# Beginning the accumulating transfers a seven sooner, and a first feed-forward block whose last pair is a seven

## The chip, the cores and the metric

The kernel runs on one core of one Trainium2 chip. The metric is the device time of one execution in microseconds (us), taken as the median of several runs. Five engines work side by side, each through its own instructions in the order in which they were written: TensorE (PE, matrix multiplications), VectorE (DVE), ScalarE (ACT), GpSimd (POOL), and SyncE (SP), which here does little else than issue loads. A transfer that is issued by SP or POOL is carried out by 16 DMA engines, which the queues share.

## The reference

One decoder layer for 256 tokens of width 2048, in float32: a SwiGLU feed-forward (half weight) with layer norm, two token mixers side by side (chunked retention, and sliding-window attention with sinks) with layer norm, a second such feed-forward with layer norm, and a gated per-layer embedding with layer norm. The change touches the two feed-forwards only, the first one most.

```python
def swiglu(x, w_gu, w_down):              # w_gu 2048 x 11264, w_down 5632 x 2048
    g, u = jnp.split(x @ w_gu, 2, axis=-1)
    return (jax.nn.silu(g) * u) @ w_down

h = x                                     # 256 x 2048
h = layer_norm(alpha * h + 0.5 * swiglu(h, w_ffn1_gu, w_ffn1_down), ln_g[0], ln_b[0])
...
h = layer_norm(alpha * h + 0.5 * swiglu(h, w_ffn2_gu, w_ffn2_down), ln_g[2], ln_b[2])
```

## The kernel before, in words

**Three products for one.** A float32 matrix is held as a rounded high part and the low rest, and a product is summed as low·high + high·high + high·low (L431 to L433, three matmuls of 128x128 by 128x512). Every weight chunk (512 KB, 128 x 1024 numbers) is loaded by SP into a slot (L119, tile `r...`), ACT casts the high part (L105, tile `h...`), and DVE subtracts it from the raw chunk for the low part (L106, tile `l...`). Slots come from one pool of 46.

**Units of a block.** The first matrix of a feed-forward (`gu`) is done in 11 blocks `j` of 512 columns of g and of u; each block sums over 8 pairs of K-chunks, and each pair is a unit. The second matrix (`down`) is done in two blocks of 22 pairs (`f1d`, then `f1e`; `f2d` and `f2e` in the second feed-forward). A string of letters gives the kinds of a block's units:

- `P`, plain: 24 matmuls; two chunks, each with a cast on ACT and a subtraction on DVE.
- `S`, a seven: seven products instead of eight (a Strassen form), so 21 matmuls. DVE forms four sums of the two chunks (L226 to L229, tiles `u` and `v`), ACT casts what comes out, and DVE makes the four low parts (`l`, `b`, `lu`, `lv`). At the end of a block that has sevens, a fold (L549 to L553) combines four extra accumulators `s0` to `s3`: ACT copies `s0`, and DVE does four sums over `evw` and `eve`. The left operands of the sevens are sums of x ("forms", L504 to L507 and a split, tiles `sums`, `f1fh`, `f1fl`), made once for a group of two pairs.
- `F`, folded: as `P`, but the low part of the second chunk isn't made by DVE. ACT writes the negated raw chunk, rounded, into the low tile (L169), POOL issues a transfer that adds the raw chunk onto it in memory (L170, an accumulating transfer), and ACT then casts the high part (L171).

**Order.** The program is written out by a planner, `fill`: it takes units from a list `plan`, loads them while their work in the queue is under a bound and slots are left, and "makes" them (casts, sums, subtractions) some time before PE needs them. `slots_for_weights` sets how many slots it may use. All engines then run strictly in the order that results. Eight PSUM banks go round: with sevens in two neighbouring blocks, the accumulators of a block use the banks that `s0` to `s3` of the block ahead of it held, so the first matmuls of a block wait for the fold of the block before.

**Start.** The first block of the first feed-forward begins while x and the weights are still arriving. x comes in four chunks, in order 0, 1, 2, 3, each ahead of the weights that meet it; block 0 takes pairs 0 to 7 as `P`, with 9 slots for weights, and 24 from unit 6 on. Both groups of forms are made at unit 7. A block without sevens is evicted with two activations and two multiplications (L1062 to L1064); one with sevens takes the fold, four additions (L1056), an activation (L1057) and a multiplication (L1058), after which the result is turned (L185 to L196).

Of the kernel before, what the change touches and what calls it, by code (L numbers as in the profile page):

```python
# [16 lines left out]
P = 128  # L17
# [34 lines left out]
SECOND_DOWN = "PPPSPSPSFSPSFSSPSPPPPP"  # L52
# [10 lines left out]
def layer(ctx: ExitStack, tc: tile.TileContext, io):  # L63
# [89 lines left out]

    class Folded:

        loads, makes, keeps, time = 1, 2, 2, 12

        def __init__(self, key):  # L160
            self.key = key

        def load(self, **how):
            self.chunk = Chunk(self.key, **how)

        def make(self):
            c = self.chunk
            c.make_hi()
            act.mul(c.lo, c.raw, -1.0)  # L169
            pool.dma_start(c.lo, c.raw, accum_op=ALU.add)  # L170
            act.copy(c.hi, c.raw)  # L171

    class Turn:
# [142 lines left out]
    def fill(must=False):  # L316

        while True:
            queued = sum(u.time for u in ready)
            left = room["slots"] - room["used"]  # L320
            wanted = must and not ready or not room["quiet"] and queued < room["ahead"]
            if loaded and wanted and loaded[0].makes <= left:
                u = loaded.pop(0)
                u.make()
                room["used"] += u.keeps - u.loads
                ready.append(u)
                continue
            first = loaded[0] if loaded else plan[0] if plan else None
            queued += sum(u.time for u in loaded)
            if plan and queued < room["far"] and plan[0].loads + first.makes <= left:  # L330
                u = plan.pop(0)
                u.load()
                room["used"] += u.loads
                loaded.append(u)
                continue
            return

    def make_next():
# [4 lines left out]
        ready.append(u)  # L343

    def take(key):
        if not ready:
            fill(True)
# [626 lines left out]
    def ffn(name, i, ht, norm, keep, residual, keepers, away):  # L974
# [33 lines left out]
        for j in range(KF // 4):  # L1008
# [22 lines left out]
            def before(u, j=j, offset=KD // 2 - len(units)):  # L1031
                u += offset
                if j == 0 and norm is None and u % 2 == 0:
                    first_chunk(u // 2)
                    if u == 6:
                        slots_for_weights(24)
                    if u == 2:
                        load_constants()
                if j == 0 and u == 7:
                    for g in sorted({p // 2 for p in SEVEN}):  # L1040
                        hi, lo = (slot([P, 8, P], F32R, f"{name}f{w}{g}") for w in "hl")
                        made[g] = seven_forms(keep[g], hi, lo)
                    if name == "f2":
                        g = AHEAD[1][0] // 2
                        made[g] = forms_of([ht[:, 4 * g : 4 * g + 4, :]], f"{name}f{g}")
# [733 lines left out]
    def first_chunk(c):  # L1779
# [4 lines left out]
        if c < 3:  # L1784
            load_x_chunk(c + 1)

# [157 lines left out]
```

## Time and profile before

| | us |
|---|---|
| median of three runs | 2230.45 |
| runs | 2227.97, 2230.45, 2230.84 |
| the profiled execution's own time | 2230.62 |
| its span, first to last instruction | 2228.6 |
| PE busy | 2218.5 |
| DVE busy | 2004.0 |
| ACT busy | 1439.0 |

The span is what the trace covers; the execution's own time is 2.0 us longer for what lies around it. Matmuls overlap (a row lists some 0.39 us, and the next starts earlier), so the pace of PE is read from the starts of neighbouring rows and not from the durations. The granted clock of PE is 0.999 over the span. In the rows of a timeline stand: start, duration, engine, line, operation, output <- inputs, shape and count, and in square brackets the idle time just ahead with what ended it. Tile names there leave out numbers: `lf_gu` is any low chunk of the first matrix of either feed-forward.

### The profile page before, as it was taken

Reading aid. Unit: us, or ns where it says so; the run is one execution under the profiler, and the core shown is the slowest. Engines: PE = TensorE matmul, PEld = TensorE weight load, DVE = VectorE, ACT = ScalarE, POOL = GpSimd, SP = SyncE. Lnnn points to the kernel's source line nnn. Section 1 sums busy time; section 2 is a strip of 40 time slices with the busy share of each in tenths; the row PEclk is TensorE's granted clock in tenths of the full one; section 3 lists DMA queues with packets and bytes.
Section 4 is the critical chain, followed back from the end, with each engine's and each line's share of the span. In section 5 each row is a group of like instructions: output and inputs, shape, how many; then the busy total and the mean of one; then the engine's idle time right before and its main releaser. Section 6 shows DMA issues by size and latency. Waiting matters only on the chain.

```text
span 2228.6 us, 29103 instructions
## 1 busy us (share of the span) xinstructions
PE 2218.5 (100%) x10140; PEld 1838.9 (83%) x10140; DVE 2004.0 (90%) x2624; ACT 1439.0 (65%) x1677; POOL 50.9 (2%) x65
## 2 busy tenths in 40 slices
PE   9999999999999999999999999999999999999998
PEld 8888888888888888888788888888888888888887
DVE  6999999989998789789999888779999999999977
ACT  6777777777565545557865567466766677765653
POOL 0000000000000000000000000000000000000000
PEclk9999999999999999999999999999999999999999
DMA  9988998976686889757976568888999999666871
GB/s 321 250 264 252 249 263 241 269 227 217 228 305 234 298 283 338 203 179 232 291 233 226 184 203 321 316 302 266 301 301 295 300 248 276 209 233 221 309 283 68
DMA packets 302075, 570.51 MB, mean 256 GB/s; under 512 B 98652, under 2 KB 103388, under 8 KB 301928
## 3 DMA queue, kind: packets, MB, share of 16 engines
q1 hardware_dynamic: 291880, 536.71, 72.3%
q0 software_dynamic: 8064, 29.36, 7.0%
q10 hardware_dynamic: 1984, 2.58, 0.4%
q8 instruction: 79, 1.29, 0.2%
q14 instruction: 68, 0.56, 0.1%
HBM read 487.32 MB, written 31.46 MB: 233 GB/s over the span
## 4 chain that ended last, share of the span: by engine, by line
PE 93%; DMA 3%; DVE 2%; issue 1%; ACT 0%; SPq 0%; ACTq 0%; POOL 0%; DVEq 0%; POOLq 0%
PE rqk L382 3%; PE f2g L431 3%; PE f2g L433 3%; PE f2g L432 3%; PE f1g L431 2%; PE f1g L433 2%; PE f1g L432 2%; PE f2u L431 2%; PE f2u L433 2%; PE f2u L432 2%; PE f1u L433 2%; PE f1u L431 2%; PE f1u L432 2%; PE aqk L382 2%; PE f2e L431 1%; PE f1e L431 1%
## 5 line engine op out<-in xcount | busy, mean ns | idle before, releaser
L106 DVE TENSOR_TENSOR lf_gu<-rf_gu,hf_gu 128x1024 fp32r<-128x1024 f32 (+1 forms) x225 | 267.7, 1210 | 22.1 <-ACT hf_gu L105 21.1
L105 ACT CAST hf_gu<-rf_gu 128x1024 fp32r<-128x1024 f32 (+1 forms) x225 | 228.7, 1039 | 22.1 <-DMA rf_gu<-in_f_gu 21.5
L106 DVE TENSOR_TENSOR lw_in_f<-rw_in_f,hw_in_f 128x1024 fp32r<-128x1024 f32 x140 | 167.8, 1219 | 15.0 <-ACT hw_in_f L105 15.0
L106 DVE TENSOR_TENSOR lf_down<-rf_down,hf_down 128x1024 fp32r<-128x1024 f32 x130 | 155.7, 1220 | 12.9 <-ACT hf_down L105 11.1
L105 ACT CAST huf_gu<-uf_gu 128x1024 fp32r<-128x1024 f32 x76 | 80.1, 1053 | 125.4 <-DVE uf_gu L227 109.4
L105 ACT CAST hf_down<-rf_down 128x1024 fp32r<-128x1024 f32 x130 | 132.7, 1049 | 30.5 <-DMA rf_down<-in_f_down 21.3
L105 ACT CAST hw_in_f<-rw_in_f 128x1024 fp32r<-128x1024 f32 x140 | 140.4, 1049 | 2.3 <-PE gt L433 1.6
L105 ACT CAST hvf_gu<-vf_gu 128x1024 fp32r<-128x1024 f32 x76 | 80.1, 1054 | 32.4 <-DVE vf_gu L229 30.5
L106 DVE TENSOR_TENSOR luf_gu<-uf_gu,huf_gu 128x1024 fp32r<-128x1024 f32 x76 | 92.6, 1218 | 0.0
L106 DVE TENSOR_TENSOR lvf_gu<-vf_gu,hvf_gu 128x1024 fp32r<-128x1024 f32 x76 | 92.6, 1218 | 0.0
L431 PE MATMUL f1g<-hf_gu,xt 128*128 128x512 f32 x232 | 90.8, 391 | 0.0
L433 PE MATMUL f1g<-lf_gu,xt 128*128 128x512 f32 x232 | 90.5, 390 | 0.0
L432 PE MATMUL f1g<-hf_gu,xt 128*128 128x512 f32 x232 | 90.5, 390 | 0.0
L431 PE MATMUL f2g<-hf_gu,ht 128*128 128x512 f32 x211 | 82.2, 390 | 0.0
L433 PE MATMUL f2g<-lf_gu,ht 128*128 128x512 f32 x211 | 82.1, 389 | 0.0
L432 PE MATMUL f2g<-hf_gu,ht 128*128 128x512 f32 x211 | 82.1, 389 | 0.0
L433 PE MATMUL f1u<-lf_gu,xt 128*128 128x512 f32 x192 | 75.0, 391 | 1.2 <-DMA lf_gu<-rf_gu 1.2
L431 PE MATMUL f1u<-hf_gu,xt 128*128 128x512 f32 x192 | 74.7, 389 | 0.0
L432 PE MATMUL f1u<-hf_gu,xt 128*128 128x512 f32 x192 | 74.7, 389 | 0.0
L170 POOL DMA_DIRECT2D lf_gu<-rf_gu x42 | 36.4, 867 | 1641.2 <-DMA rf_gu<-in_f_gu 1017.6
L105 ACT CAST huf_down<-uf_down 128x1024 fp32r<-128x1024 f32 x32 | 33.7, 1054 | 60.7 <-DVE uf_down L227 58.7
L1057 ACT ACTIVATE eve<-eve 128x1024 f32<-128x1024 f32 x20 | 21.2, 1061 | 67.3 <-DVE eve L1056 67.3
(1512 smaller groups left out, 6978.3 us busy)
## 6 DMA issues: line engine op xcount, KB each, us to landing
rf_gu<-in_f_gu SPq DMA_DIRECT2D x361, 512.0 KB
rf_down<-in_f_down SPq DMA_DIRECT2D x176, 512.0 KB
rw_in_f<-in_w_in_f SPq DMA_DIRECT2D x148, 512.0 KB
lf_gu<-rf_gu POOLq DMA_DIRECT2D x42, 512.0 KB, 8.2
rw_rv<-in_w_rv SPq DMA_DIRECT2D x32, 512.0 KB
rw_ret<-in_w_ret SPq DMA_DIRECT2D x32, 512.0 KB
rw_mix<-in_w_mix SPq DMA_DIRECT2D x32, 512.0 KB
rw_pg<-in_w_pg SPq DMA_DIRECT2D x32, 512.0 KB
```

The lines of the kernel that those rows point to most:

```text
L105: act.copy(dst_hi, src)
L106: (lo_engine or dve).tensor_tensor(dst_lo, src, dst_hi, ALU.subtract)
L170: pool.dma_start(c.lo, c.raw, accum_op=ALU.add)
L382: pe.matmul(ps[f], hi[:, kk, f * P : (f + 1) * P], rhs(k), start=k == 0, stop=k == n_k - 1,)
L431: pe.matmul(o, al, bh, start=first, stop=False)
L432: pe.matmul(o, ah, bh, start=False, stop=False)
L433: pe.matmul(o, ah, bl, start=False, stop=self.left == 0)
L1057: act.activation(g, g, AF.Silu)
```

## The change

1. The accumulating transfer of an `F` is split off. A unit `Folding` (load, negation, transfer) is put into the plan ahead of the work it follows, by at least 12 of the planner's matmul units and back to the start of a seven where one is near; a unit `Folded` at the old place only casts the high part.
2. Block 0 of the first feed-forward takes pairs 0, 1, 4, 5, 6, 7, 2 as `P` and then pair 3 as a seven. x is loaded in order 0, 2, 3, 1. The forms of group 1 are made at unit 6, those of group 0 at unit 7. The slots go from 9 to 16 at unit 4 and to 28 at unit 6.
3. Block 1 of the first feed-forward is `FFSSFSSF` and not `FFSSFSSP`.
4. The first `down` block of both feed-forwards has another order, with six `F` instead of five and eight `S` as before.

```diff
+FOLD_AHEAD = 12, 12
+FORMS_AT = {"f1": {6: (1,), 7: (0,)}, "f2": {7: (0, 1, 2)}}
+FIRST_SLOTS = {4: 16, 6: 28}
+X_ORDER = (0, 2, 3, 1)
+FIRST_UNITS = {
+    "f1": [('P', 0), ('P', 1), ('P', 4), ('P', 5), ('P', 6), ('P', 7), ('P', 2), ('S', 3)],
+    "f2": [('P', 0), ('P', 1), ('P', 2), ('P', 3), ('P', 4), ('P', 5), ('P', 6), ('P', 7)],
+}
-FIRST_DOWN = "PPPPPPFFSFSPSFSPSFSSPS"
+FIRST_DOWN = "PPPPPFFSFSFSPSFSPSFSPS"
...
-    class Folded:
-        loads, makes, keeps, time = 1, 2, 2, 12
+    class Folding:
+        loads, makes, keeps, time = 1, 1, 2, 0
...
         def make(self):
             c = self.chunk
-            c.make_hi()
+            c.lo = slot(list(c.raw.shape), F32R, "l" + c.name)
             act.mul(c.lo, c.raw, -1.0)
             pool.dma_start(c.lo, c.raw, accum_op=ALU.add)
+
+    class Folded:
+        loads, makes, keeps, time = 0, 1, 2, 12
...
+        def make(self):
+            c = self.chunk = self.begun.chunk
+            c.hi = slot(list(c.raw.shape), F32R, "h" + c.name)
             act.copy(c.hi, c.raw)
+            room["used"] -= self.begun.keeps
+
+    def fold_at(ahead, key):
+        begun = Folding(key)
+        at, time = len(plan), 0
+        while at > 0 and time < ahead:
+            at -= 1
+            time += plan[at].time
+        if ahead and any(isinstance(u, Seven) for u in plan[at - 12 : at + 1]):
+            while not isinstance(plan[at], Seven):
+                at -= 1
+        plan.insert(at, begun)
+        plan.append(Folded(begun))
...
             elif kind == "F":
-                plan.extend(of(keys(n, p)) for n, of in enumerate((Single, Folded)))
+                plan.append(Single(keys(0, p)))
+                fold_at(FOLD_AHEAD[keys(1, p)[0][-3:] == "_gu"], keys(1, p))
...
         if j == 0:
-            return [("P", p) for p in range(KD // 2)]
+            return FIRST_UNITS[name]
...
+        if name == "f1" and j == 1:
+            return units_of("FFSSFSSF", SEVEN)
...
-                    if u == 6:
-                        slots_for_weights(24)
+                    if u in FIRST_SLOTS:
+                        slots_for_weights(FIRST_SLOTS[u])
...
-                if j == 0 and u == 7:
-                    for g in sorted({p // 2 for p in SEVEN}):
+                for g in FORMS_AT[name].get(u, ()) if j == 0 else ():
+                    if g < 2:
...
-            load_x_chunk(c + 1)
+            load_x_chunk(X_ORDER[c + 1])
```

The lines of the new kernel are shifted: casts and subtractions are L118 and L119, loads L132, the negation and its transfer L181 and L182, the later cast L198, the sums of a seven L267 to L270, forms L544 to L547, the fold L589 to L593, the eviction L1097 to L1099.

The first place is DVE at the end of block 0 of the first feed-forward. In a name such as `lf1_gu_0_0_3_429` the letter says what it is (`r` raw, `h` high, `l` low, `u` and `v` the sums of a seven, `b` its fourth operand), and after `f1_gu` stand the block, the half (0 for g, 1 for u), the pair and a tile number. Before:

```order
L106 TENSOR_TENSOR f1fl1_448<-sums_449,f1fh1_447 128x1024
L106 TENSOR_TENSOR lf1_gu_1_0_5_469<-rf1_gu_1_0_5_413,hf1_gu_1_0_5_468 128x1024
L1064 TENSOR_TENSOR f1v0_493<-f1v0_493,f1u00_119 128x512
L1064 TENSOR_TENSOR f1v0_493<-f1v0_493,f1u01_120 128x512
L226 TENSOR_TENSOR uf1_gu_1_0_0_518<-rf1_gu_1_0_0_417,rf1_gu_1_1_0_419 128x512
```

And now:

```order
L119 TENSOR_TENSOR f1fl0_468<-sums_469,f1fh0_467 128x1024
L119 TENSOR_TENSOR lf1_gu_1_0_5_498<-rf1_gu_1_0_5_447,hf1_gu_1_0_5_497 128x1024
L590 TENSOR_TENSOR evw_510<-eve_509,f10s1_122 128x512
L591 TENSOR_TENSOR eve_509<-evw_510,f10s2_123 128x512
L592 TENSOR_TENSOR evw_510<-f10s3_124,evw_510 128x512
L593 TENSOR_TENSOR evw_510<-f10s3_124,eve_509 128x512
L1097 TENSOR_TENSOR eve_509<-eve_509,f1g00_117 128x512
L1097 TENSOR_TENSOR eve_509<-eve_509,f1g01_118 128x512
L1097 TENSOR_TENSOR evw_510<-evw_510,f1u00_119 128x512
L1097 TENSOR_TENSOR evw_510<-evw_510,f1u01_120 128x512
L1099 TENSOR_TENSOR evw_510<-eve_509,evw_510 128x1024
L267 TENSOR_TENSOR uf1_gu_1_0_0_542<-rf1_gu_1_0_0_449,rf1_gu_1_1_0_451 128x512
```

The two multiplications (L1064) have become nine instructions: four of the fold, four additions, one multiplication. The sums of the first seven of block 1 stand behind all of them. Ahead of the rows shown stand now the work of the seven of block 0, the low part of a chunk of block 1 (`lf1_gu_1_0_4`) and the four sums for the forms of group 0.

The second place is ACT over the same stretch. Before:

```order
L105 CAST hf1_gu_1_0_4_407<-rf1_gu_1_0_4_405 128x1024
L169 ACTIVATE lf1_gu_1_1_4_434<-rf1_gu_1_1_4_411 128x1024
L171 CAST hf1_gu_1_1_4_433<-rf1_gu_1_1_4_411 128x1024
L105 CAST f1fh0_438<-sums_440 128x1024
L105 CAST f1fh1_447<-sums_449 128x1024
L105 CAST hf1_gu_1_0_5_468<-rf1_gu_1_0_5_413 128x1024
L169 ACTIVATE lf1_gu_1_1_5_489<-rf1_gu_1_1_5_415 128x1024
L171 CAST hf1_gu_1_1_5_488<-rf1_gu_1_1_5_415 128x1024
L1062 ACTIVATE f1v0_493<-f1g00_117 128x512
```

And now, first where the seven of block 0 begins, then, behind the other three casts of that seven, up to the eviction:

```order
L118 CAST hf1_gu_0_1_2_367<-rf1_gu_0_1_2_343 128x1024
L181 ACTIVATE lf1_gu_1_1_4_383<-rf1_gu_1_1_4_345 128x1024
L181 ACTIVATE lf1_gu_1_1_5_386<-rf1_gu_1_1_5_347 128x1024
L118 CAST f1fh1_401<-sums_403 128x1024
L118 CAST hf1_gu_0_0_3_428<-rf1_gu_0_0_3_349 128x1024
```

```order
L118 CAST hf1_gu_1_0_4_443<-rf1_gu_1_0_4_353 128x1024
L198 CAST hf1_gu_1_1_4_465<-rf1_gu_1_1_4_345 128x1024
L118 CAST f1fh0_467<-sums_469 128x1024
L118 CAST hf1_gu_1_0_5_497<-rf1_gu_1_0_5_447 128x1024
L198 CAST hf1_gu_1_1_5_501<-rf1_gu_1_1_5_347 128x1024
L589 COPY eve_509<-f10s0_121 128x512
L1098 ACTIVATE eve_509<-eve_509 128x1024
```

Both negations now stand ahead of the cast of the first forms, and the copy that frees the bank of `s0` stands behind the cast of the forms of group 0 and of four chunks of block 1. On SP the loads 17 to 22 are now 0_2 and 1_2 of block 0, 1_4 and 1_5 of block 1, then 0_3 and 1_3 of block 0 (half and pair), and 0_4 of block 1 behind them.

The third place is DVE before the end of the first `down` block of the first feed-forward, ahead of its last seven, pair 19. Before:

```order
L106 TENSOR_TENSOR lvf1_down_0_18_4896<-vf1_down_0_18_4879,hvf1_down_0_18_4895 128x1024
L106 TENSOR_TENSOR lf1_down_0_21_4914<-rf1_down_0_21_4911,hf1_down_0_21_4913 128x1024
L106 TENSOR_TENSOR lf1_down_1_21_4941<-rf1_down_1_21_4938,hf1_down_1_21_4940 128x1024
L226 TENSOR_TENSOR uf1_down_0_19_4969<-rf1_down_0_19_4965,rf1_down_1_19_4967 128x512
L227 TENSOR_TENSOR uf1_down_0_19_4969<-rf1_down_1_19_4967 128x512
```

And now:

```order
L119 TENSOR_TENSOR lvf1_down_0_18_4931<-vf1_down_0_18_4914,hvf1_down_0_18_4930 128x1024
L119 TENSOR_TENSOR lf1_down_0_21_4953<-rf1_down_0_21_4876,hf1_down_0_21_4952 128x1024
L119 TENSOR_TENSOR lf1_down_1_21_4971<-rf1_down_1_21_4934,hf1_down_1_21_4970 128x1024
L267 TENSOR_TENSOR uf1_down_0_19_4995<-rf1_down_0_19_4936,rf1_down_1_19_4938 128x512
L268 TENSOR_TENSOR uf1_down_0_19_4995<-rf1_down_1_19_4938 128x512
```

The work of DVE reads alike, but the tiles are numbered as the planner hands them out: the raw chunks of pair 19 had 4965 and 4967, behind both low parts of pair 21, and now have 4936 and 4938, ahead of them. They take slots that the pair before gives back, 18 matmuls sooner. In all, PE has 9954 rows instead of 9957, DVE 2572 instead of 2562, ACT 1555 instead of 1550, POOL 73 instead of 70.

More of the change, by code (lines that the diff above doesn't have):

```diff
@@ L322, in fill @@
             if loaded and wanted and loaded[0].makes <= left:
[L323 to L326, printed above, removed]
+                make_next()
                 continue
@@ L342, in make_next @@
         room["used"] += u.keeps - u.loads
-        ready.append(u)
+        if u.time:
+            ready.append(u)
     def take(key):
-        if not ready:
+        while not ready:
             fill(True)
@@ L1034, in before @@
                     first_chunk(u // 2)
[L1035 to L1036 removed]
+                    if u in FIRST_SLOTS:
+                        slots_for_weights(FIRST_SLOTS[u])
                     if u == 2:
                         load_constants()
[L1039 to L1040 removed]
+                for g in FORMS_AT[name].get(u, ()) if j == 0 else ():
+                    if g < 2:
                         hi, lo = (slot([P, 8, P], F32R, f"{name}f{w}{g}") for w in "hl")
                         made[g] = seven_forms(keep[g], hi, lo)
[L1043 to L1044 removed]
+                    else:
                         made[g] = forms_of([ht[:, 4 * g : 4 * g + 4, :]], f"{name}f{g}")
```

8 lines of the change are left out of this document (6 added, 2 removed).

## The prediction

> **What bounds the kernel now.** I read the page's first part, then the waits of PE, then the timeline at each of them.
>
> ```profile
> PE 2218.5 (100%) x10140; PEld 1838.9 (83%) x10140; DVE 2004.0 (90%) x2624; ACT 1439.0 (65%) x1677; POOL 50.9 (2%) x65
> PE f1u L433 <- DMA lf_gu<-rf_gu: 1.2, 2, 0.9
> PE f1e L431 <- DVE evw L550: 0.6, 1, 0.6
> PE mr1a L433 <- DVE lw_ret L106: 0.5, 1, 0.5
> PE f2e L431 <- DVE evw L550: 0.5, 1, 0.5
> ```
>
> PE sets the end: of a span of 2228.6 us it is busy 2218.5. What a change can win is therefore matmuls left out, and the waits of this short list (total, times, longest, in us). The change reaches three of its rows: two accumulating transfers that land late in the first feed-forward, and the fold at the end of the first `down` block in each feed-forward.
>
> The pace is read from a unit of 24 matmuls without a wait, the last of block 0:
>
> ```profile
> 44.65 0.39 PE L431 MATMUL f1g<-hf_gu,xt 128*128 128x512 f32 x1
> 50.09 0.39 PE L431 MATMUL f1g<-hf_gu,xt 128*128 128x512 f32 x1
> ```
>
> (50.09 − 44.65) / 24 = 0.2267 us for one. What a wait costs beyond its idle time is seen here:
>
> ```profile
> 73.43 0.39 PE L432 MATMUL f1u<-hf_gu,xt 128*128 128x512 f32 x1
> 74.70 0.50 PE L433 MATMUL f1u<-lf_gu,xt 128*128 128x512 f32 x1 [0.88 <-DMA lf_gu<-rf_gu]
> 75.04 0.39 PE L431 MATMUL f1u<-hf_gu,xt 128*128 128x512 f32 x1
> 574.81 0.39 PE L433 MATMUL f1e<-lf_down,f1ah 128*128 128x512 f32 x1
> 575.79 0.50 PE L431 MATMUL f1e<-hf_down,f1al 128*128 128x512 f32 x1 [0.59 <-DVE evw L550]
> ```
>
> From 73.43 to 75.04 are 1.61 us for two steps, so 1.61 − 2 × 0.2267 = 1.16 is lost: the idle 0.88, and 0.28 of refilling the pipeline. With the same 0.28, the other late transfer costs 1.2 − 0.88 + 0.28 = 0.60, the fold of `f1` 0.59 + 0.28 = 0.87, that of `f2` 0.5 + 0.28 = 0.78. All four: 3.41 us.
>
> **Late transfers, removed.** The chain of waits names what ends late:
>
> ```profile
> 63.73 10.93 DMA lf_gu<-rf_gu
> 558.00 5.72 DMA rf_down<-in_f_down
> ```
>
> The first row is the accumulating transfer of block 1's third `F`; issued at 63.73, it lands at 74.66, right where PE waits. Its negation now stands about a seven's worth of casts earlier. I work out the issue at about 64.7 from the ACT order below and not much sooner, because block 1 itself will run late; but PE needs it later too: where it asked at 73.66, it asks at 73.66 + 2.1 + 0.95 − 0.68 = 76.0 (the terms are worked out below). By the 8.2 us that the page gives as the median to landing, or the 10.93 of this row, it lands at 72.9 to 75.6. The wait goes. The other one, later in the first feed-forward, was 0.3 long, and its transfer begins a seven sooner without any lateness ahead of it; it goes too: −1.76. If it doesn't, these 1.76 stay (a rival below).
>
> **Fold of the `down` blocks, removed.** DVE at the end of `f1d`:
>
> ```profile
> 558.19 2.35 DVE L106 TENSOR_TENSOR lf_down<-rf_down,hf_down 128x1024 fp32r<-128x1024 f32 x2
> 563.84 0.69 DVE L226 TENSOR_TENSOR uf_down<-rf_down,rf_down 128x512 f32<-128x512 f32 x1 [3.29 <-DMA rf_down<-in_f_down]
> 575.05 0.68 DVE L550 TENSOR_TENSOR evw<-eve,f1d0s 128x512 f32<-128x512 f32 x1
> ```
>
> DVE stands still for 3.29 us for the load of the last seven (the load of the chain, 558.00 + 5.72), and the whole queue behind it, to the fold at 575.05, is late by that; PE misses it by 0.59. In the new order this load takes slots given back 18 matmuls, 18 × 0.2267 = 4.1 us, sooner. It lands near 559.6, the low parts before it end at 560.5, and the fold starts near 571.7, over 3 us before PE asks. Late next there would be the low parts of the second block, which stand ahead of the fold and move with it. −0.87 and, by the same rows in the second feed-forward, −0.78. Six `F` instead of five take one low part (2.35 / 2 = 1.17 us of DVE) from each of the two blocks and put a transfer on POOL's queue instead; where no wait stands, that is worth nothing.
>
> **Three matmuls, removed.** The seven of block 0 has 21 matmuls instead of 24: −3 × 0.2267 = −0.68.
>
> **The end of block 0, added.** This is the term on which the sum hangs. PE would end block 0 at 44.65 + 21 × 0.2267 = 49.41, and block 1 starts in the bank of `s0`, which ACT has to copy first. I place the instructions of the new order by hand, with the landings and durations of these rows:
>
> ```profile
> 35.36 1.05 ACT L105 CAST hf_gu<-rf_gu 128x1024 fp32r<-128x1024 f32 x1 [0.90 <-DMA rf_gu<-in_f_gu]
> 36.66 1.06 ACT L105 CAST hf_gu<-rf_gu 128x1024 fp32r<-128x1024 f32 x1 [0.26 <-DMA rf_gu<-in_f_gu]
> 38.01 1.06 ACT L169 ACTIVATE lf_gu<-rf_gu 128x1024 fp32r<-128x1024 f32 x1 [0.28 <-DMA rf_gu<-in_f_gu]
> 45.35 1.05 ACT L105 CAST hf_gu<-rf_gu 128x1024 fp32r<-128x1024 f32 x1
> 46.30 1.05 ACT L169 ACTIVATE lf_gu<-rf_gu 128x1024 fp32r<-128x1024 f32 x1
> 83.12 0.58 ACT L549 COPY eve<-f11s 128x512 f32<-128x512 f32 x1
> 38.90 0.42 DVE L504 TENSOR_TENSOR sums<-xraw 128x256 f32<-128x256 f32 x1
> 40.02 0.43 DVE L507 TENSOR_TENSOR sums<-xraw,sums 128x256 f32<-128x256 f32 x1
> 50.96 0.68 DVE L226 TENSOR_TENSOR uf_gu<-rf_gu,rf_gu 128x512 f32<-128x512 f32 x1
> 53.62 1.22 DVE L106 TENSOR_TENSOR lf_gu<-rf_gu,hf_gu 128x1024 fp32r<-128x1024 f32 x1
> 54.76 0.69 DVE L106 TENSOR_TENSOR bf_gu<-rf_gu,bf_gu 128x512 fp32r<-128x512 f32 x1
> 55.36 1.22 DVE L106 TENSOR_TENSOR luf_gu<-uf_gu,huf_gu 128x1024 fp32r<-128x1024 f32 x1
> 57.63 0.68 DVE L226 TENSOR_TENSOR uf_gu<-rf_gu,rf_gu 128x512 f32<-128x512 f32 x1
> ```
>
> The first three rows start when a load lands. The loads of 512 KB keep their places in SP's queue, so the 21st and 22nd, now the two chunks of the seven, land at 36.66 and 38.01, and the one before them, the second to be negated, at 35.36. ACT waits for it with the cast of the first forms queued behind: negation to 36.4, forms to 37.4. DVE then takes, each from start to start: their low part 1.14 (53.62 to 54.76), to 38.57; the four sums of the seven 2.66 (50.96 to 53.62), to 41.23; its low parts 1.14 + 0.60 + 1.13 + 1.14 (54.76, 55.36, and half of the rest to 57.63), to 45.24, which PE needs no sooner than about 46; a low part of block 1, to 46.38; four sums for forms, 1.12 + 0.43, to 47.93. Only then does ACT cast these forms (48.0), two chunks of block 1 at a spacing of 0.95 (46.30 − 45.35), and at 50.85 copy `s0` in 0.58. PE starts block 1 at about R = 51.5 and not at 49.41: **+2.1**. In general R is 12.9 us behind the start of the sums of the seven, which is 38.6 or the landing of its second chunk, if that is later.
>
> What is late next is DVE, which now does fold, additions and a multiplication before the first sums of block 1:
>
> ```profile
> 84.18 0.69 DVE L550 TENSOR_TENSOR evw<-eve,f11s 128x512 f32<-128x512 f32 x1 [1.22 <-PE f11s L433]
> 86.90 1.22 DVE L106 TENSOR_TENSOR lf_gu<-rf_gu,hf_gu 128x1024 fp32r<-128x1024 f32 x1
> 88.87 1.36 DVE L1056 TENSOR_TENSOR eve<-eve,f1g 128x512 f32<-128x512 f32 x2 [0.76 <-PE f1g L433]
> 93.06 1.23 DVE L1058 TENSOR_TENSOR evw<-eve,evw 128x1024 f32<-128x1024 f32 x1
> 94.20 0.69 DVE L226 TENSOR_TENSOR uf_gu<-rf_gu,rf_gu 128x512 f32<-128x512 f32 x1
> ```
>
> Fold 2.72 (84.18 to 86.90), two pairs of additions 2 × 1.3, multiplication 1.14 (93.06 to 94.20): the first sums start at R + 6.5, where before they started at 50.96, 0.9 behind PE's 50.09. A seven takes DVE 57.63 − 50.96 = 6.67, and PE 21 × 0.2267 = 4.76. The two `F` ahead give PE 48 matmuls = 10.9 us. The first seven is in time (its `lu` at R + 12.0, needed R + 13.4). The second has its low part at R + 6.5 + 6.67 + 2.66 + 1.14 = R + 17.0, and PE asks for it with its third matmul at R + 10.9 + 4.76 + 0.45 = R + 16.1: 0.95 lost. The `F` behind it lets DVE catch up in part; the last seven needs its `lu` and `lv` early and loses about 1.1 by the same count. **+2.05** in block 1. After that the lag is gone, since DVE waits for PE at the next boundary as before (0.76 in the row of 88.87). From below these two terms are bounded by 0, if the copy comes before 49.41; from above by the rival with late loads. I take the middle, as the chain is made of rows with one place for error, the landings.
>
> **Sum**, against the profiled execution's own 2230.62: −1.76 − 0.87 − 0.78 − 0.68 + 2.1 + 2.05 = +0.06, so 2230.7. The median of the runs is 0.17 lower; I leave the sum as it is and say 2230.6. The change wins about 4 us and gives 4 back at the start.
>
> **Rivals.** *B, faster:* the end of block 0 costs nothing. PE then gains all terms: 2230.62 − 4.09 = 2226.5. For it speaks that this takes only 2 us in a chain of a dozen steps, and that more slots from unit 4 on can bring loads forward; against it, that the DMA engines have nothing left to give there:
>
> ```profile
> 7.00:50.00 43.00, 43.00 (x189) 34.99 (x188) 31.39 (x34) 29.70 (x32) 1.87 (x2) 1.00 1.00 345
> ```
>
> (the last two numbers: a DMA share of 1.00, at 345 GB/s).
>
> *C, slower:* the accumulating transfers, now issued at about 34.5 and 36.5, take DMA time from the loads of the seven of block 0.
>
> ```profile
> q0 software_dynamic: 8064, 29.36, 7.0%
> 39.39 1.01 POOL L170 DMA_DIRECT2D lf_gu<-rf_gu  x1 [38.08 <-ACT lf_gu L169]
> q1 hardware_dynamic: 803, 1.55, 104.3%
> q0 software_dynamic: 142, 0.52, 68.5%
> ```
>
> POOL's queue takes 7.0% of 2228.6 us for 29.36 MB, or 56 transfers of 512 KB: 2.8 us of all engines each. One that is ahead of the chunk landing at 38.01 moves it to 40.8, which by the rule above makes R 2.2 later: 2232.9; both: 2235.7. It decides from a landing after 38.6. Against it: the transfer issued at 39.39 moved nothing in the window 39.4 to 43.4 (third row, only SP's queue) and took 68.5% in the window from 43.4 to 47.2 (fourth row). With the same 4 us, transfers issued at 34.5 and 36.5 start at 38.5 and later, just behind that landing; the margin is half a microsecond.
> The Trainium skill ("DMA: Bandwidth & Descriptors", section "Queues, rings and completion order") says that each DMA engine goes round between the queues it has work for, packet by packet. By that rule a transfer in POOL's queue would share from the moment its packets are there, which is rival C; the 4 us without a packet of it here speak for a late beginning, and the shares after it agree with the rule.
>
> *D:* the change doesn't do what it says, and the old waits stay. With the late transfers 2230.6 + 1.76 = 2232.4; with the folds too, + 1.65 = 2234.0. For it: POOL's queue is in order, and landings vary (8.2 to 10.93 above). Against it: the load of pair 19 comes 4.1 us sooner where 0.6 is missing.
>
> **Chances.** The forecast 0.47, with a range of its own from 2229 to 2232.5 (a microsecond on the landing is one on R); B 0.20; C 0.20, about half of it with both transfers; D 0.13. The range from 2225.8 to 2236.0 takes in B and all of C and D. A measurement of this kernel can tell about 0.2% (4.5 us) from no change: faster means below 2226.0, slower above 2234.9. B ends 0.5 above the first bound, and the runs of before differ by 2.9, so about half of B counts as faster, with a little of the rest: 0.12. Slower are C with both transfers and waits that I haven't seen, 0.18. The rest, 0.70, is the same.
>
> **What would show it.** Right: PE's waits of the first feed-forward list a wait for the copy `eve` of about 2 us near 49.4 and two of about 1 us in block 1, for `lf_gu` and for `luf_gu` or `lvf_gu`; the waits for DMA `lf_gu` and for DVE `evw` in `f1e` and `f2e` are gone. The sums of the seven of block 0 begin at 38.6, and POOL's first transfers are issued near 34.5 and 36.5. Wrong: no wait for `eve` (B), the sums begin after 40 with the second chunk named as releaser (C), the old rows stay (D), or any new wait in the blocks 2 to 10, where I expect none.

## The result, and the profile after

| | before | after |
|---|---|---|
| median of 16 runs, us | 2228.12 | 2234.73 |
| lowest to highest, us | 2226.10 to 2233.15 | 2229.32 to 2256.31 |
| the profiled execution's own time, us | 2230.62 | 2231.57 |

The change makes the kernel slower by a third of a per cent: the ratio is 1.0035, with a 95% interval from 1.0024 to 1.0046. That is 6.6 us in the median, more than the 4.5 us by which the prediction would tell a change. The median lies inside the wide range that was given (2225.8 to 2236.0) and outside the forecast's own (2229 to 2232.5). One execution further down, the 2278.55 us of plain_first, counts as a slow one: it stands in that run's median and range and not in its ratio, and without it the median is 2250.55. The traces disagree with the runs: the profiled execution of the new kernel took only 0.95 us longer than that of the old one, near what was forecast. The runs of before lie within 7 us, those of after within 27. So the first thing to explain is not where this one trace spends its time, but what happens in the executions that it doesn't show.

First what the trace of the changed kernel does show. The rows of its list of PE's waits that lie in the first feed-forward (total, times, longest, us):

```profile
PE f1g L470 <- ACT eve L589: 2.1, 1, 2.1
PE f11s L472 <- DVE lf_gu L119: 0.6, 1, 0.6
PE f11s L472 <- DVE luf_gu L119: 0.3, 1, 0.3
PE f11s L472 <- DVE lvf_gu L119: 0.2, 1, 0.2
```

All four rows were forecast (the last two as one), and none of the old ones (`lf_gu` by DMA, `evw` in `f1e` and `f2e`) is left. The timelines of DVE, ACT, PE and DVE again, at the end of block 0:

```profile
38.57 0.68 DVE L267 TENSOR_TENSOR uf_gu<-rf_gu,rf_gu 128x512 f32<-128x512 f32 x1
50.93 0.58 ACT L589 COPY eve<-f10s 128x512 f32<-128x512 f32 x1
51.55 0.50 PE L470 MATMUL f1g<-hf_gu,xt 128*128 128x512 f32 x1 [2.09 <-ACT eve L589]
57.97 0.69 DVE L267 TENSOR_TENSOR uf_gu<-rf_gu,rf_gu 128x512 f32<-128x512 f32 x1
```

The sums of the seven start at 38.57 (worked out: 38.57), the copy at 50.93 (50.85), block 1 at 51.55 (51.5), its first sums 6.4 later (6.5). But one wait is missing from that list, because it took only 0.03 us. In the timeline of PE, block 3:

```profile
158.64 0.39 PE L471 MATMUL f1u<-hf_gu,xt 128*128 128x512 f32 x1
159.06 0.50 PE L472 MATMUL f1u<-lf_gu,xt 128*128 128x512 f32 x1
```

Here PE takes 0.42 us for a step of 0.2267. The low part that it needs comes from an accumulating transfer that was issued at 144.52 and landed at 159.02, 14.5 us later and just in time, although it had begun a seven sooner. In the trace of before no accumulating transfer takes more than 10.93.

### The profile page after: what moved, and what is told of

It reads as the page before. It is cut to its first block, busy times and chain, and to the rows that moved or that the text cites. A ratio compares the mean times of both kernels' runs of the same rounds, so it can differ in the third digit from the quotient of the medians.

```text
span 2229.8 us, 29140 instructions
## 1 busy us (share of the span) xinstructions
PE 2218.6 (99%) x10137; PEld 1838.0 (82%) x10137; DVE 2008.0 (90%) x2634; ACT 1442.6 (65%) x1682; POOL 53.5 (2%) x68
## 4 chain that ended last, share of the span: by engine, by line
PE 93%; DVE 4%; DMA 1%; issue 1%; ACT 1%; SPq 0%; ACTq 0%; DVEq 0%
PE rqk L421 3%; PE f2g L470 3%; PE f2g L471 3%; PE f2g L472 3%; PE f1g L470 2%; PE f1g L472 2%; PE f1g L471 2%; PE f2u L470 2%; PE f2u L471 2%; PE f2u L472 2%; PE f1u L472 2%; PE f1u L470 2%; PE f1u L471 2%; PE aqk L421 2%; PE f1e L472 1%; PE f2d L472 1%
## 5 line engine op out<-in xcount | busy, mean ns | idle before, releaser
L119 DVE TENSOR_TENSOR lf_gu<-rf_gu,hf_gu 128x1024 fp32r<-128x1024 f32 (+1 forms) x223 | 265.9, 1210 | 31.9 <-ACT hf_gu L118 31.1
L118 ACT CAST hf_gu<-rf_gu 128x1024 fp32r<-128x1024 f32 (+1 forms) x223 | 227.0, 1038 | 30.3 <-DMA rf_gu<-in_f_gu 28.3
L119 DVE TENSOR_TENSOR lw_in_f<-rw_in_f,hw_in_f 128x1024 fp32r<-128x1024 f32 x140 | 167.8, 1220 | 15.8 <-ACT hw_in_f L118 15.6
L119 DVE TENSOR_TENSOR lf_down<-rf_down,hf_down 128x1024 fp32r<-128x1024 f32 x128 | 154.0, 1220 | 19.2 <-ACT hf_down L118 17.4
L118 ACT CAST hf_down<-rf_down 128x1024 fp32r<-128x1024 f32 x128 | 131.7, 1049 | 42.1 <-DMA rf_down<-in_f_down 19.6
L118 ACT CAST huf_gu<-uf_gu 128x1024 fp32r<-128x1024 f32 x77 | 81.1, 1053 | 99.9 <-DVE uf_gu L268 92.5
L118 ACT CAST hw_in_f<-rw_in_f 128x1024 fp32r<-128x1024 f32 x140 | 140.4, 1049 | 2.3 <-PE gt L472 1.6
L118 ACT CAST hvf_gu<-vf_gu 128x1024 fp32r<-128x1024 f32 x77 | 81.2, 1055 | 31.6 <-DVE vf_gu L270 30.2
L119 DVE TENSOR_TENSOR luf_gu<-uf_gu,huf_gu 128x1024 fp32r<-128x1024 f32 x77 | 93.9, 1219 | 0.0
L119 DVE TENSOR_TENSOR lvf_gu<-vf_gu,hvf_gu 128x1024 fp32r<-128x1024 f32 x77 | 93.9, 1219 | 0.0
L182 POOL DMA_DIRECT2D lf_gu<-rf_gu x43 | 37.3, 868 | 1640.8 <-ACT lf_gu L181 1271.2
L118 ACT CAST huf_down<-uf_down 128x1024 fp32r<-128x1024 f32 x32 | 33.7, 1053 | 53.0 <-DVE uf_down L268 47.1
```

The source lines that it names most:

```text
L118: act.copy(dst_hi, src)
L119: (lo_engine or dve).tensor_tensor(dst_lo, src, dst_hi, ALU.subtract)
```

## The experiments

Each run is compared with the kernel before on the same chip. The last column is the longest time from POOL's issue of an accumulating transfer to its landing, in that run's one trace.

| run | median us | lowest to highest | before | ratio, 95% interval | longest landing |
|---|---|---|---|---|---|
| after_again | 2232.89 | 2231.07 to 2249.27 | 2228.74 | 1.0029 (1.0015 to 1.0043) | 21.6 |
| plain_first | 2251.83 | 2234.37 to 2278.55 | 2228.74 | 1.0092 (1.0066 to 1.0117) | 22.5 |
| seven_alone | 2237.47 | 2236.42 to 2238.91 | 2228.74 | 1.0041 (1.0028 to 1.0054) | 11.0 |
| no_ahead | 2242.08 | 2240.71 to 2248.07 | 2228.74 | 1.0069 (1.0057 to 1.0081) | 10.8 |
| after_turn_later | 2241.22 | 2234.27 to 2243.76 | 2228.61 | 1.0049 (1.0036 to 1.0061) | 12.0 |
| before_turn_later | 2251.45 | 2249.62 to 2258.10 | 2228.61 | 1.0109 (1.0096 to 1.0122) | 20.4 |
| plain_turn_later | 2237.97 | 2235.50 to 2240.15 | 2228.61 | 1.0042 (1.0030 to 1.0054) | 16.6 |
| down_only | 2228.16 | 2226.43 to 2229.86 | 2228.61 | 0.9998 (0.9990 to 1.0007) | 10.7 |
| third_late | 2234.35 | 2232.17 to 2235.05 | 2228.58 | 1.0025 (1.0015 to 1.0035) | 11.2 |
| plain_third_late | 2229.54 | 2227.99 to 2234.22 | 2228.58 | 1.0008 (0.9999 to 1.0017) | 11.4 |
| after_copied | 2230.24 | 2228.71 to 2232.39 | 2228.99 | 1.0007 (0.9998 to 1.0016) | 11.3 |
| plain_copied | 2226.68 | 2225.22 to 2227.89 | 2228.99 | 0.9988 (0.9979 to 0.9997) | 13.0 |

A ratio can differ by some 0.001 (2 us) from the quotient of the medians, since it weighs the runs otherwise; differences of 1 or 2 us between two rows are not to be pressed.

### Which part costs: four runs

**after_again** is the changed kernel itself.

> The changed kernel once more, for a second trace. The profiled execution of it was 1 us longer than that of before, while its runs lie 6.6 us higher in the median and spread over 16 us (those of before over 7 us). Theory L (landings): the seven of block 0 starts when its second chunk lands; 38.0 us was a lucky landing, 0.6 us ahead of the point at which it decides, and in most executions it lands later and PE waits longer for the copy of s0. Then this trace has, if its time is t, a wait for the copy eve of about 2.1 + (t - 2231.6) us, and the sums of that seven are released by the load. Theory F (transfers begun early): the accumulating transfers, a seven earlier, disturb loads in later blocks in some executions. Then the wait for eve stays at 2.1 and what t has above 2231.6 lies in waits for DMA in the blocks 1 to 10 or in the down blocks. Theory C (collision at the start): as L, but the chunk is late because the two early accumulating transfers move before it has landed. Ratio for all three 1.002 to 1.005.

Its profiled execution took 2240.98 us, 9.4 more than the first one. Its waits of PE:

```profile
PE f1u L472 <- DMA lf_gu<-rf_gu: 8.0, 2, 7.1
PE f1g L470 <- ACT eve L589: 1.7, 1, 1.7
```

The longest of them by the chain of waits, in block 3 (start, us, what):

```profile
144.47 21.55 DMA lf_gu<-rf_gu
166.02 0.04 issue
166.07 0.80 PE f1u L472
```

The wait for `eve` is no longer than in the other trace, so theory L, late landings at the start, doesn't carry these 9.4 us. The transfer that was just in time in the first trace is 7.1 us late in this one: theory F's kind of row.

**plain_first** takes the seven of block 0 back and keeps the early transfers.

```diff
-X_ORDER = (0, 2, 3, 1)
+X_ORDER = (0, 1, 2, 3)
-FIRST_SLOTS = {4: 16, 6: 28}
+FIRST_SLOTS = {6: 24}
-    "f1": [('P', 0), ('P', 1), ('P', 4), ('P', 5), ('P', 6), ('P', 7), ('P', 2), ('S', 3)],
+    "f1": [('P', 0), ('P', 1), ('P', 2), ('P', 3), ('P', 4), ('P', 5), ('P', 6), ('P', 7)],
```

(and both groups of forms at unit 7)

> The first block plain again, with x in order, its forms and its slots as before; transfers begun early, block 1 and the down blocks as changed. Theories L and C: the old waits are gone and nothing is added, 3.4 us less than before, ratio 0.9985 (0.997 to 0.9995), with the spread of before. Theory F: the loss stays, ratio 1.002 or more.

It is the other way round: without the seven the kernel is 20 to 23 us slower than before (by the ratio, and by the medians). Its waits of PE:

```profile
PE f1u L472 <- DMA lf_gu<-rf_gu: 11.4, 2, 8.2
PE f11s L472 <- DVE lf_gu L119: 4.9, 1, 4.9
PE f11s L470 <- ACT hf_gu L118: 1.8, 1, 1.8
```

And its chain of waits in block 7:

```profile
318.99 22.54 DMA lf_gu<-rf_gu
341.53 0.04 issue
```

Theories L and C fall as the main cause: by both, the loss would have gone with the seven. Something in the early transfers is worth tens of us in some orders and little in others.

**seven_alone** is the kernel before with the new first block and nothing else: the changed kernel with these edits. **no_ahead** has the first of them alone.

```diff
-FOLD_AHEAD = 12, 12
+FOLD_AHEAD = 0, 0
-FIRST_DOWN = "PPPPPFFSFSFSPSFSPSFSPS"
+FIRST_DOWN = "PPPPPPFFSFSPSFSPSFSSPS"
-            return units_of("FFSSFSSF", SEVEN)
+            return units_of("FFSSFSSP", SEVEN)
```

> Only the first block is changed (last pair as a seven, x in another order, forms, slots); accumulating transfers begin as before, block 1 and the down blocks as before. The seven's loads then stand two places earlier in the queue and the early transfers behind them. Theory L: the terms of the prediction (2.1 + 2.05 - 0.68) and late landings on top, ratio 1.002 to 1.004, spread wider than before. Theory C: no collision, the terms alone, 1.0015, spread as before. Theory F: at most 1.0015.

> The change without the early beginning: each accumulating transfer is issued right after its chunk's place as before, the rest as changed. Theory L: as the changed kernel and the two old waits for late transfers (1.8 us) back, ratio 1.003 to 1.005. Theories C and F: the disturbance is gone, ratio 1.001 to 1.002, and the wait for eve stays near 2 us in the trace.

Waits of PE of the one and of the other:

```profile
PE f1u L472 <- DMA lf_gu<-rf_gu: 4.9, 3, 3.0
PE f1g L470 <- ACT eve L589: 2.7, 1, 2.7
PE f10s L470 <- DVE f1fl L119: 1.6, 1, 1.6
```

```profile
PE f1u L472 <- DMA lf_gu<-rf_gu: 5.5, 3, 3.2
PE f1d L472 <- DMA lf_down<-rf_down: 3.0, 1, 3.0
PE f2d L472 <- DMA lf_down<-rf_down: 1.9, 1, 1.9
```

No landing is long in either (11.0 and 10.8), and their runs lie close together, but both are slower than the change as a whole. The parts lean on each other: the seven makes block 1 late on ACT and DVE, so that transfers of old timing come late there (in either trace two of the three waits for `lf_gu` lie in block 1, 4.0 and 3.9 us), and the new order of the `down` blocks has an `F` that is late (3.0 and 1.9) unless it begins early. The early beginning repairs that, and brings long landings of its own. What F didn't say is why they are long in some blocks only.

### What makes a landing long: three groups of runs

The timelines of SP and POOL in block 3, before, and after (first trace):

```profile
140.80 2.91 SPq L189 DMA_TRANSPOSE mf<-wf  x1
147.81 0.87 POOL L170 DMA_DIRECT2D lf_gu<-rf_gu  x1 [17.74 <-ACT lf_gu L169]
```

```profile
143.23 4.89 SPq L230 DMA_TRANSPOSE mf<-wf  x1
144.52 0.86 POOL L182 DMA_DIRECT2D lf_gu<-rf_gu  x1 [25.68 <-DVE lvf_gu L119]
```

Every finished block is turned by a transposing transfer in SP's queue. Before, POOL issued the third accumulating transfer of a block about 7 us behind it (3.6 to 6.3 in the later blocks of the first feed-forward); now it is 1.1 to 1.3 us behind in blocks 1 to 5, and in the later ones up to 4 us ahead. What the queues moved, before in the window 147.5 to 157.5, and in after_again in the window 147 to 157:

```profile
q1 hardware_dynamic: 1313, 2.54, 73.5%
q0 software_dynamic: 144, 0.52, 29.3%
```

```profile
DMA packets 2035, 0.96 MB, mean 96 GB/s; under 512 B 1855, under 2 KB 1855, under 8 KB 2034
q1 hardware_dynamic: 1969, 0.71, 107.1%
q0 software_dynamic: 65, 0.24, 28.2%
```

(packets, MB, share of 16 engines; the first window begins 0.3 us ahead of POOL's issue and the second 2.5 us behind it). Behind the transposing transfer an accumulating one moves all its 144 packets in the window. Beside it, 65 in the same 10 us, among 1855 packets of under 512 bytes; and the engines, though busy, move 96 GB/s in all. A packet of POOL's queue is on record for 0.282 × 160 / 65 = 0.69 us instead of 0.293 × 160 / 144 = 0.33 (such records can overlap on an engine: the shares of the two queues here come to 135%). The Trainium skill ("DMA: Bandwidth & Descriptors", section "Queues, rings and completion order") has each DMA engine go round between its queues packet by packet. Both queues move packets in the second window, as that rule has it; the doubled time of a packet is not in that rule.

From this theory M: the early transfers are slow because they meet the transposing ones. First the transposing transfers are moved, and the accumulating ones left:

```diff
-DELAY = 1
+DELAY = 3
```

in the changed kernel (**after_turn_later**), in the kernel before (**before_turn_later**), and in plain_first (**plain_turn_later**).

> The changed kernel with the transposing transfer of each finished block two jobs of the side list later (some 7 us); accumulating transfers where the change puts them. Theory M (they meet the transposing transfer): in the changed kernel POOL issues the first accumulating transfer of a block 1 to 1.5 us behind the issue of the transposing one (143.2 and 144.5, 184.6 and 185.6), both then move slowly side by side (25 to 90 GB/s for 6 to 16 us), and the accumulating one lands 14 to 22 us after its issue where it took at most 10.9 before. With the transposing one moved away the long landings go (none over 12 us), PE has no wait for an accumulating transfer, the spread shrinks, and the time is that of the prediction's sum, 2226 to 2231 us, ratio 0.999 to 1.001. Rival E (too early in itself: the transfer competes with loads, whatever else moves): the landings stay, ratio 1.002 to 1.004.

> The other way round: the kernel before, its transposing transfers two jobs later, so that they come within 1 or 2 us of the third accumulating transfer of each block instead of 7 us ahead of it. Nothing begins earlier here. Theory M: landings of 14 us and more appear, with waits of PE for them of several us, ratio 1.003 or more, and a wider spread. Theory E: nothing happens, ratio within 0.999 to 1.001.

> The first block plain, the rest as changed, and the transposing transfers two jobs later. With the transposing transfers where they were, this was 23 us slower than before, with landings of 17.6 and 22.5 us. Theory M: those landings go, and what was expected of the plain first block comes out, the old waits gone and no new ones: 2225 to 2228, ratio 0.9985 (0.997 to 0.9995). Theory E: still 1.005 or more.

The second of these is the clear one. Nothing begins earlier in it, two accumulating transfers now meet transposing ones badly, and the kernel is 23 us slower. Its waits of PE:

```profile
PE f2u L433 <- DMA lf_gu<-rf_gu: 11.7, 1, 11.7
PE f1u L433 <- DMA lf_gu<-rf_gu: 8.1, 1, 8.1
```

And its chain of waits in block 10, where the turn was issued at 429.85:

```profile
432.10 16.84 DMA lf_gu<-rf_gu
448.93 0.04 issue
```

Other meetings in that run, 0.4 to 1.7 us behind the turn in blocks 1 to 6, landed in 6.8 to 8.2 us, as three of five did in the first trace of the changed kernel. So being close makes a long landing possible, and not certain. It doesn't look like mere chance: in both traces of the changed kernel it is the same two transfers that take long, those of blocks 3 and 4 (14.5 and 14.3 us, then 21.6 and 15.4). In after_turn_later the landings go (12.0 at most) and PE waits for no accumulating transfer, as M says, but the time misses the forecast by 10 us. Of its waits of PE the two longest, and then a window of 2 us:

```profile
PE f1g L470 <- ACT eve L589: 2.9, 1, 2.9
PE f28s L472 <- DVE lf_gu L119: 1.6, 1, 1.6
```

```profile
54.00:56.00 2.00, 2.00 (x7) 1.44 (x6) 1.86 (x4) 0.00 (x0) 0.00 (x0) 0.59 1.06 354
```

Sevens of the second feed-forward are late on DVE (`f28s` and others), and behind the longer wait for `eve` PE runs at a clock of 0.59 (third number from the right of the window's row; 7 matmuls in 2 us). The eleven waits for such sevens come to 5.1 us, some 8 with their refill; with 0.8 us more for `eve` and 1.6 for the slow clock (estimates from this trace) that is about the 10.3 us by which this profiled execution is longer than the first one of the changed kernel. The wait for `eve` is no price of the moved turn, since the first turn is issued only at 67.7: the second chunk to be negated landed at 37.06 here. That moving the turn is what makes DVE late in the second feed-forward is likely, and not shown. plain_turn_later falls from 2251.8 to 2238.0, so most of plain_first's loss goes with the turn; what stays is one meeting in the second feed-forward, where a landing takes 16.6 us and a load beside it holds ACT, with the copy `eve` in its queue; PE waits 6.3 us for it (timeline of ACT):

```profile
1735.69 1.04 ACT L118 CAST hf_gu<-rf_gu 128x1024 fp32r<-128x1024 f32 x1 [11.45 <-DMA rf_gu<-in_f_gu]
1739.03 0.57 ACT L589 COPY eve<-f26s 128x512 f32<-128x512 f32 x1
```

Then the turns stay and only the meeting transfer goes back: from block 2 on (**third_late**, the changed kernel), or from block 1 on (**plain_third_late**, with the first block plain and block 1 as before).

```diff
-                fold_at(FOLD_AHEAD[keys(1, p)[0][-3:] == "_gu"], keys(1, p))
+                gu = keys(1, p)[0][-3:] == "_gu"
+                late = gu and keys(1, p)[1] >= 2 and 0 < at < 6 and units[at - 1][0] == "S"
+                fold_at(0 if late else FOLD_AHEAD[gu], keys(1, p))
```

> The changed kernel, but from block 2 of the first feed-forward on the third accumulating transfer of a block (the one that is issued just behind the transposing transfer) goes back to its old place, some 7 us behind the transposing one. All others begin early, and no transposing transfer is moved. Theory M: no landing over 13 us in the first feed-forward, waits of PE for DMA under 1 us in all, the waits of blocks 0 and 1 as in the changed kernel (2.1 for eve, 1.1 for the sevens), 2229 to 2232 us, ratio 1.0005 to 1.0015, spread of 5 us or less. Rival E (beginning early disturbs in itself, the first two transfers as much as the third): long landings and waits of several us stay, ratio 1.002 to 1.004.

> The same with the first block plain and block 1 as before the change, and the third transfer late in block 1 too; the down blocks as changed. Theory M: neither the collisions nor the cost of the seven, old fold waits gone, up to 1.8 us of the old late transfers left: 2226 to 2228.5, ratio 0.9985 to 1.0000, a version not slower than either kernel. Theory E: 1.002 or more, like the plain first block with all transfers early, only less.

Both lose their long landings (11.2 and 11.4), though two of the three transfers of a block still begin early, where rival E would keep them long. The runs of third_late lie within 2.9 us, where the changed kernel's lie within 27 and 18. But its median is no lower than that of the changed kernel, and 2 us above what was expected: here the spread goes and the time stays. Its trace has other rows for that. Waits of PE:

```profile
PE f1g L470 <- ACT eve L591: 2.9, 1, 2.9
PE f2u L472 <- DMA lf_gu<-rf_gu: 1.5, 1, 1.5
```

Timeline of ACT:

```profile
35.86 1.06 ACT L181 ACTIVATE lf_gu<-rf_gu 128x1024 fp32r<-128x1024 f32 x1 [0.29 <-DMA rf_gu<-in_f_gu]
51.62 0.58 ACT L591 COPY eve<-f10s 128x512 f32<-128x512 f32 x1
```

A window behind that copy:

```profile
52.00:54.00 2.00, 1.75 (x4) 1.46 (x5) 1.85 (x4) 0.20 (x1) 0.00 (x0) 0.56 1.05 389
```

The load of the second chunk to be negated landed at 35.86 here and at 35.18 in the first trace of the changed kernel, and the copy stands 0.69 us later, 51.62 and not 50.93: the chain from landing to copy is stiff. In the five traces that have both the seven and the early transfers, that landing comes between 34.6 and 37.1, and the copy 15.5 to 15.8 behind it, so a milder form of theory L holds: the start differs by some 2 us from trace to trace. The wait of 2.9 is again followed by half the clock, for some 3 us. The late transfer of 1.5 us lies in the second feed-forward. plain_third_late is 1 us above before; two late transfers of 1.9 and 1.4 us are left in its trace.

Last, the transposing transfers are replaced by plain copies of the same bytes in the same place, in the changed kernel (**after_copied**) and in plain_first (**plain_copied**). The blocks of the two feed-forwards are then not turned.

```diff
+            if self.name[:2] in ("f1", "f2"):
+                sync.dma_start(
+                    self.moved.rearrange("p h a b n -> p (h a b n)"), self.words.rearrange("p h a n -> p (h a n)")
+                )
+                return
             sync.dma_start_transpose(
```

> The changed kernel, but in the two feed-forwards the transposing transfers are plain copies of the same bytes, at the same places of the queue; the blocks are then not turned, so the output is another. What this tells apart: whether the accumulating transfers are slowed by the transposing ones as such, or by anything that stands at that place of SP's queue. Theory M: no landing over 13 us, PE waits for DMA under 0.5 us in all, the waits of blocks 0 and 1 stay (1.7 to 2.9 for eve), spread of 5 us or less, 2229 to 2234 us, ratio 1.0005 to 1.0025. Rival Q (any transfer at that place, or the loads behind it): landings of 14 us and more stay, ratio 1.002 to 1.004 with the spread of the changed kernel.

> The same with the first block plain and every accumulating transfer of the first feed-forward early, the version that was 23 us slower with the transposing transfers. Here, too, the blocks are not turned. Theory M: the 23 us go altogether, no wait for an accumulating transfer over 0.5 us, none for eve: 2223 to 2228 us, ratio 0.998 to 0.9995. Rival Q: 1.004 or more.

Rival Q falls. The changed kernel comes out at 2230.24 us with a spread of 3.7, and plain_first, which was 23 us slower than before, is 2.3 us faster. The longest waits of after_copied, and that of plain_copied (without the wait for `ident` at the start, which every run has):

```profile
PE f1g L475 <- ACT eve L594: 1.7, 1, 1.7
PE f11s L477 <- DVE lf_gu L119: 0.6, 1, 0.6
```

```profile
PE f1g L475 <- ACT hf_gu L118: 0.7, 1, 0.7
```

No wait for an accumulating transfer is left in either. The two differ by the seven of block 0 and what goes with it: 2230.24 − 2226.68 = 3.6 us. The kernel before was not run with copies, so what a copy saves by itself, apart from the meetings, isn't known.

**down_only** has the new order of the `down` blocks, with transfers early there alone, and everything else as before: plain_first with these edits.

```diff
-FOLD_AHEAD = 12, 12
+FOLD_AHEAD = 12, 0
-            return units_of("FFSSFSSF", SEVEN)
+            return units_of("FFSSFSSP", SEVEN)
```

> Only the order of the first down blocks is changed, and the accumulating transfers begin early in the down blocks alone, where no block is being turned. Both theories: the two waits for the fold are gone (1.65 us) and the two late transfers of the first feed-forward stay: 2226 to 2228, ratio 0.999 (0.9985 to 1.0000), spread as before. If the early beginning costs something even there, 1.001 and waits for lf_down.

0.9998, not to be told from no change. Both waits for the fold are gone from its list, and two for an accumulating transfer are left:

```profile
PE f1u L472 <- DMA lf_gu<-rf_gu: 0.7, 1, 0.7
...
PE f2u L472 <- DMA lf_gu<-rf_gu: 0.3, 1, 0.3
```

Only plain_copied came out faster than the kernel before, by 0.1%, and its blocks are not turned. Of the versions with the right output none is faster; this is the nearest one.

## Why the prediction was right and wrong

- **Three matmuls and the end of block 0: right.** +2.1, +2.05 and −0.68 make 3.5 us; the two copied kernels, where no accumulating transfer is late, differ by 3.6. In the trace the wait for `eve` with its refill is 51.55 − 49.08 − 0.23 + 0.11 = 2.35 (0.11 for the slower step behind it), and the three waits of block 1 with theirs come to about 1.9. One term was added up wrongly: R + 17.0 less R + 16.1 is 0.9 and not 0.95.
- **The fold waits: right in the traces, not to be told in the runs.** They went in all traces with the new `down` order and early transfers there. But the margin of "over 3 us" was wrong. Timeline of the changed kernel, first trace, DVE and then PE:

```profile
573.22 2.36 DVE L119 TENSOR_TENSOR lf_down<-rf_down,hf_down 128x1024 fp32r<-128x1024 f32 x2 [1.68 <-ACT hf_down L118]
575.49 0.68 DVE L590 TENSOR_TENSOR evw<-eve,f1d0s 128x512 f32<-128x512 f32 x1
576.69 0.39 PE L470 MATMUL f1e<-hf_down,f1al 128*128 128x512 f32 x1
```

The first sum of the fold ends at 576.17, 0.5 us ahead of the matmul that needs it. DVE waits 1.68 us for a cast that ACT begins only when PE has done with a product (572.11), and ACT's copy of `s0` stands at 574.85, behind PE's last product in it. In the trace of before that copy began at 572.51 for the same reason, so the 571.7 that was worked out for the fold could not be reached. In the runs down_only is 0.45 us below before, and its interval (2.2 us less to 1.6 more) holds nothing as well as the 1.65.
- **The base was a bad one.** The profiled execution of before, 2230.62, is 1.6 to 2.5 us above the medians of 16 to 21 runs of it (2228.1 to 2229.0). That the waits to be won were smaller in most executions than in that trace is likely, and not shown, as there is no second trace of it. Without meetings, plain_copied wins 2.3 us where 3.4 were worked out.
- **The late transfers: here it failed.** The step was: "its transfer begins a seven sooner without any lateness ahead of it; it goes too". It took the time to landing, 8.2 to 10.93 us, as belonging to the transfer, wherever it begins. The runs show that it belongs to the place: a seven sooner is beside the transposing transfer, and there, 0.2 to 1.3 us behind it, the landing is anything from 7 to 22.5 us. The old late transfers did go; new ones came in other blocks. That the first trace nonetheless ended 0.95 us from before, near the forecast, is luck: the transfer of block 3 landed just in time in it and 7.1 us late in the second. The last line of the prediction named the sign, a new wait in blocks 2 to 10, but gave it no mechanism and, with other unseen waits, a part of 0.18.
- **Rivals C and D.** C had the right kind of event, a transfer that meets another on the DMA engines, and the wrong partner: it had the early transfers slow down the loads of block 0. Those stayed on time: the copy came at 50.93. D's 2234.0 lies next to the measured median by accident, since its waits are gone in both traces.
- **The account.** Against the kernel before on the same chip, the change costs 6.6 us in the first series and 4.2 in after_again, and 1.25 with copies in place of the turns (3.5 lost in blocks 0 and 1, some 2.3 won). As an estimate, then, the meetings with the transposing transfers cost 2.9 to 5.4 us in the median; the slowest execution, 2256.31, lies 26 above after_copied's median. The estimate is not a clean one, for want of a run of the kernel before with copies. What the runs show is that the meetings make the long landings and the spread. Of the median, a part is the start: third_late has no long landing, and still lies 5.8 us above before, of which some 2.4 are its later `eve` and the slow clock behind it.

## What to carry to other kernels

A transfer that is moved keeps its bytes and not its duration: look up what stands in the other queues at its new place, above all transfers of small packets, and take the duration from the nearest one that has met such company. A wait of 0.03 us in a trace is a margin of nothing, and several executions show what one trace can't: a wider spread of the runs is itself a finding. And where one part of a change repairs what another breaks, undoing them singly gives times that can't be added up.

## What the runs showed of the hardware

- Two transfers side by side, one accumulating and one transposing, were together slower than one behind the other. In 20 us around the turn of block 2, the kernel before (138 to 158) and the changed one in its first trace (141 to 161):

```profile
DMA packets 4560, 5.56 MB, mean 278 GB/s; under 512 B 2238, under 2 KB 2238, under 8 KB 4558
DMA packets 3906, 4.32 MB, mean 216 GB/s; under 512 B 2198, under 2 KB 2198, under 8 KB 3905
```

In after_again it is 138 GB/s from 141 to 161. How much they slow each other differed from execution to execution at the same distance: 14.5 and 21.6 us for the same transfer, issued 1.3 us behind the turn. What decides it stays open.
- PE's clock fell to about half behind all waits of 2.9 us and more (0.56 and 0.59 in the windows above, some 3 us long; about 1.6 us lost, 8 matmuls at 0.43 us and not 0.23). Below that the length alone doesn't decide: the waits of 2.7 for `eve` in seven_alone and of 2.6 in no_ahead left the clock at 1.00, but behind the wait of 1.9 for `lf_down` in no_ahead it was 0.50 for 3 us, and likewise behind one of 1.8 in plain_first. The Trainium skill ("TensorE: Matmul & The Clock Gate", Part 1) gives an idle window of about 3.4 us that runs freely; here waits of little more than half that length were sometimes enough.
